# Softmax sums of heads A and B applied at the output projection of a two-layer hybrid decoder

## Chip, cores and metric

One core of one Trainium2 chip runs the whole program. The metric is device time in microseconds (us) of one execution, as the median of several runs.

## What is computed

Two decoder layers on x of shape (1, 1024, 1024), all in float32. In each layer the normalized input is projected once, and three groups of attention heads use the columns: six dilated-window heads A (width 64), six latent-attention heads B (value width 64) and four differential heads C. Their outputs stand side by side (features 0 to 383 from A, 384 to 767 from B, 768 to 1023 from C), are multiplied by `w_o` and added to x. A feed-forward block with a squared ReLU follows. What matters here:

```python
s = jnp.where(valid, s, NEG)
lse = jax.nn.logsumexp(s, axis=-1)
p = jnp.exp(s - lse[..., None])
out = jnp.einsum('bgnqk,bgnkd->bgnqd', p.astype(v.dtype), vv)
...
mixed = jnp.concatenate([out_a, out_b, out_c], axis=-1)
x = x + mixed @ w_o[layer]
```

For A and B each row of exponentials is divided by its sum. The kernel folds the three windows of A into one mask with logarithms of multiplicities, so that A, too, is one softmax for each query.

## The kernel before, in words

The function `tile_trunk` does not issue instructions. It records them (`nc` is a Recorder) with the engines on which each may run, and `Recorder.order` (line 256) then sets the order of every engine by a list schedule with a cost for each operation and a rank that is the place in the program plus a bias. The SyncE queue (SP), which issues all DMAs, is ordered by the same planner. Tiles have a tag with a fixed number of slots (`SLOTS`, line 32), and the tiles of one tag are handed out strictly in the order of the program. PSUM's eight banks are shared by the tags of `BANKS`. Matrix products are made of three passes (high by high, high by low, low by high part), so every operand is split: a "hi" copy rounded to fp32r and a "lo" difference. `WAYS` (line 50) says which engines may do each kind: `hi` is GpSimd (POOL), `lo` is VectorE (DVE) or POOL, `osum` is ScalarE (ACT), `oadd` is POOL.

A layer goes through these stages: the projection of the input (chunks of columns, most of them worked on beside the heads), 16 heads in the order A0, A1, C0 to C3, A2 to A5, B0 to B5, the output projection, and the feed-forward block.

Each head has four groups g of two query tiles i of 128 rows. `scores` (line 804) makes the products q k on TensorE (PE), subtracts from the mask and takes the row minimum on DVE, and takes the exponential on ACT, which also leaves the sum of the row (line 826). For A and B, DVE then takes the reciprocal of that sum (line 829) and POOL multiplies the row of probabilities `p` with it (kind `norm`, line 830). `values` (line 849), one group later, transposes `p` on PE (tiles `ptp`), splits it into `ph` and `pl`, and multiplies it with v into the bank `o`, of which partitions 0 to 63 and 64 to 127 hold two halves of the sum. After each second group `o_sum` (line 892) copies the two halves out with two ACT copies (`ot`, `od`), adds them on POOL and stores the 64 rows of that head to `mix_dram` with one DMA.

The output projection reads the features in blocks f of 128 (A is f = 0 to 2, B is 3 to 5, C is 6 and 7; a block holds two heads), in the groups (6, 0), (7, 1), (2, 3, 4), (5). `project_load` (line 1195) loads for each f two halves `mixr` of 128x512 with one DMA each, into the tag `pp` (5 slots, which `ph` and `pl` of the heads use as well), and splits each into `mixh` and `mixl`. The first two groups run beside the B heads. The third and fourth are loaded behind all heads in the order of the program (line 1320), and the first half of their products, for the token tiles t = 0 to 3, fills eight PSUM banks: 24 matmuls for each f, 96 in all (lines 1322 to 1329). The feed-forward block needs their sums.

Of the kernel before, what the change touches and what calls it, by code (L numbers as in the profile page):

```python
# [46 lines left out]
LAG = 3  # L47
DEEP = 6000.0

WAYS = {'hi': 'g', 'hiact': 's', 'lo': 'vg', 'lop': 'g', 'evac': 'sv', 'norm': 'g', 'osum': 's', 'oadd': 'g', 'lsc': 'gs', 'rope': 'v', 'sq': 's', 'fadd': 'gv', 'fhi': 'sg', 'flo': 'vg', 'fnorm': 'sg', 'fevac': 'sv', 'fsnap': 's', 'fsq': 'sv'}  # L50
SHARED = 0.5

BLOCKS = (0, 4, 8, 12, 15)
# [368 lines left out]
def tile_trunk(  # L422
# [21 lines left out]
    def bank(tag, name):  # L444
        return nc.tile(psum, [P, 512], F32, name, tag, BANKS[tag], True)
# [76 lines left out]
    hl_dram = nc.tile(dram, [DEPTH * NT, P, D], F32, "hl_dram")  # L522
    cq_dram = nc.tile(dram, [DEPTH * S, 512], F32, "cq_dram")
    mix_dram = nc.tile(dram, [DEPTH * D, S], F32, "mix_dram")

    def rstd_of(y, ssq, n, eps, w, nm):

# [45 lines left out]
    for L in range(DEPTH):  # L573
# [230 lines left out]
        def scores(hd, g):  # L804
# [5 lines left out]
            def piece(i, mi, z, c0, m):  # L810
# [11 lines left out]
                                               scalar=w[:, 0:1] if z else BIG, op0=ALU.add, op1=ALU.min, accum_out=w[:, z:z + 1])  # L822
                if c0 + m < W:
                    return
                tot = hd["tot"][mi][:, i] if "tot" in hd else w[:, 2:3]
                nc.scalar.activation(p, p, AF.Exp, bias=w[:, z:z + 1], scale=-1.0, accum_out=tot)
                if mi == 0:
                    if coef is None:
                        nc.vector.reciprocal(w[:, 3:4], tot)
                        copy("norm", p, p, w[:, 3:4])  # L830
                    hd["P"][g][i % 2] = p
                else:

                    prev = hd["P"][g][i % 2]
                    nc.vector.reciprocal(w[:, 3:4], tot)
                    nc.vector.scalar_tensor_tensor(w[:, 4:5], w[:, 3:4], hd["tot"][0][:, i], coef, ALU.mult, ALU.mult)
                    nc.vector.scalar_tensor_tensor(prev, p, w[:, 4:5], prev, ALU.mult, ALU.add)
# [54 lines left out]
        def o_sum(g, o, f, par, nm):  # L892

            tmp = tl("oo", [P, 512], f"ot_{nm}_{g}")
            rows = slice(64 * par, 64 * par + 64)
            dst = tl("oo", [P, 512], f"od_{nm}_{g}")[rows, :] if f < 6 else mix_tile(f, g)[rows, :]
            copy("osum", tmp[rows, :], o[64:128, :])
            copy("osum", dst, o[0:64, :])
            pair("oadd", dst, dst, tmp[rows, :], ALU.add)
            if f < 6:  # L900
                mix_out(f, g, dst, 64 * par, 64)

        def fin_mix(f, par, nm):
            return lambda g, o: o_sum(g, o, f, par, nm)

        def mask_a(W, c0, m):
            return maska[:, S - W + c0:S - W + c0 + m]
# [7 lines left out]
        def prep_a(h):  # L915
# [14 lines left out]
            def keys(cs, pt):  # L930
                hi_act(k1s[:, cs], pt)
                for z in range(2):
# [3 lines left out]
            q = turned(f"q{nm}", two(qa), lambda cs, pt: hi_act(qs[:, cs], pt))  # L936
            bl = zipped(k[0], k[1], q[0], q[1])
            return bl, dict(maps=[([(qs, k1s), (qs, k2s)], None)], mask=mask_a, scale=SC_A, nm=nm, P={},
                            v=make_v(va[:, :, c], par, nm), fin=fin_mix(i, par, nm))


        bx = {}
# [136 lines left out]
        def prep_b(h):  # L1079
            i, j = h // 2, h % 2  # L1080
            nm = f"B{L}{h}"
            qh, ql = [z[:96] for z in pairs[i][0][j]]
            kh, kl = [Halves(*z) for z in pairs[i][1][j]]
            return [], dict(maps=[([(qh, kh), (qh, kl), (ql, kh)], None)], mask=mask_c, scale=SC_B, nm=nm, P={}, cut=512,
                            v=make_v(bx["V"][:, :, 64 * h:64 * h + 64], j, nm), fin=fin_mix(3 + i, j, nm))

        cst = {}

# [106 lines left out]
        def project_load(gi):  # L1195
# [7 lines left out]
            for f in groups[gi]:  # L1203
# [4 lines left out]
                ml = tl(tag, [P, S], f"mixl_{L}_{f}", F32R)  # L1208
                for z in range(2):
                    cs = slice(z * 512, (z + 1) * 512)  # L1210
                    raw = tl("pp", [P, 512], f"mixr_{L}_{f}_{z}")
                    nc.sync.dma_start(raw, mix_dram[L * D + f * P:L * D + (f + 1) * P, cs])
                    hi_pool(mh[:, cs], raw)
                    lo_dve(ml[:, cs], raw, mh[:, cs])
                mx.append((mh, ml))
# [504 lines left out]
```

## Time and profile before

| | |
|---|---|
| median of 3 runs | 2548.02 us (2547.39 to 2551.18) |
| the profiled execution, its own time | 2549.46 us |
| its span from the first to the last instruction | 2547.7 us |
| PE busy | 2473.8 us, 97% |
| weight loads (PEld) busy | 2077.0 us, 82% |
| DVE busy | 2069.9 us, 81% |
| ACT busy | 1238.3 us, 49% |
| POOL busy | 920.2 us, 36% |
| mean granted TensorE clock | 0.991 |

The heads of the first layer run from about 65 to 587 us, those of the second from about 1320 to 1845 us. The granted clock is a share of full speed. PE's busy time is a union of pipelined instructions, each of which lasts longer than the distance to the next, so an instruction's own duration is not what it takes from PE.

### The profile page before, as it was taken

To read this page: it belongs to the slowest core of one execution; us is meant where nothing else is said; L and a number is where in the kernel's file an instruction comes from. 1 tells how busy PE (TensorE), PEld (TensorE's weight loads), DVE (VectorE), ACT (ScalarE), POOL (GpSimd) and SP (SyncE) were. 2 spreads that over 40 slices of the span, in tenths; PEclk is the share of its full clock that TensorE was granted. 3 is DMA by queue.
4 is the path that set the end of the run, shared out by engine and by line. 5 is a ranking of instruction groups with operands and counts; after the bars stand their busy time and mean duration, and the time that the engine had idled before them with its cause. 6 is when DMAs were issued, how large, how long until landed. Compare 5 with 4: busy or idle time off the path is not lost. (4 is left out here: it accounts for less than half of the span.)

```text
span 2547.7 us, 39227 instructions
## 1 busy us (share of the span) xinstructions
PE 2473.8 (97%) x12808; PEld 2077.0 (82%) x12808; DVE 2069.9 (81%) x4326; ACT 1238.3 (49%) x2548; POOL 920.2 (36%) x1078
## 2 busy tenths in 40 slices
PE   8999999999999999999999999999999999999996
PEld 7878889988788887888888778898887888788885
DVE  4679998887877777989856799988778777789989
ACT  3566667743544444323235666677345444333332
POOL 2344355653200114455323343556330001144543
PEclk9999999999999999999999999999999999999998
DMA  8354433433354457544453554344243444765332
GB/s 255 96 142 135 112 94 94 135 93 130 116 172 164 153 197 262 156 145 120 137 164 97 133 137 122 81 110 142 78 142 129 163 159 146 268 210 157 112 120 79
DMA packets 292636, 360.58 MB, mean 142 GB/s; under 512 B 48848, under 2 KB 172112, under 8 KB 292432
## 3 DMA queue, kind: packets, MB, share of 16 engines
q1 hardware_dynamic: 292432, 358.08, 45.6%
q8 instruction: 102, 1.67, 0.3%
q14 instruction: 102, 0.84, 0.1%
HBM read 231.63 MB, written 94.90 MB: 128 GB/s over the span
## 5 line engine op out<-in xcount | busy, mean ns | idle before, releaser
L418 PE MATMUL pd<-hb,ha 128*128 128x512 f32 x2520 | 577.2, 390 | 5.4 <-DVE hb L418 3.5
L418 PE MATMUL pu<-xc,uh 128*128 128x512 f32 x1792 | 552.7, 393 | 13.4 <-ACT ua L418 8.2
L418 PEld LDWEIGHTS pd<-hb,ha 128*128 128x128 f32 x2520 | 471.4, 188 | 109.6 <-DVE hb L418 8.3
L418 PEld LDWEIGHTS pu<-xc,uh 128*128 128x128 f32 x1792 | 336.9, 189 | 90.0 <-ACT ua L418 10.0
L418 PE MATMUL pu<-xc,ul 128*128 128x512 f32 x896 | 346.7, 393 | 0.0
L418 PEld LDWEIGHTS pu<-xc,ul 128*128 128x128 f32 x896 | 169.6, 189 | 36.8 <-DVE ul L418 0.8
L418 DVE TENSOR_TENSOR ha<-hr,ha 128x512 fp32r<-128x512 f32 x151 | 145.6, 967 | 24.8 <-POOL ha L418 23.0
L418 POOL TENSOR_SCALAR ha<-hr 128x512 fp32r<-128x512 f32 x90 | 74.1, 824 | 245.1 <-DVE xd L418 94.8
L418 ACT ACTIVATE hb<-wt 128x512 fp32r<-128x512 f32 x98 | 60.4, 627 | 184.4 <-PE pd L418 157.3
L418 ACT ACTIVATE uh<-su 128x512 fp32r<-128x512 f32 x124 | 77.5, 631 | 138.4 <-PE pu L418 121.6
L418 ACT ACTIVATE hb<-wd 128x512 fp32r<-128x512 f32 x82 | 50.4, 627 | 158.8 <-PE pd L418 157.3
L418 ACT ACTIVATE p_C<-p_C,w_C 128x256 f32<-128x256 f32 (+7 forms) x128 | 98.9, 773 | 55.3 <-DVE w_C L418 54.7
L418 POOL TENSOR_SCALAR p_A<-p_A,w_A 128x128 f32<-128x128 f32 (+3 forms) x96 | 77.2, 806 | 116.5 <-DVE w_A L418 83.6
L418 POOL TENSOR_SCALAR uh<-wu 128x512 fp32r<-128x512 f32 x16 | 13.3, 832 | 280.1 <-PE pu L418 168.5
L418 DVE TENSOR_TENSOR hb<-wt,hb 128x512 fp32r<-128x512 f32 x105 | 109.7, 1061 | 0.7 <-ACT hb L418 0.5
L418 DVE TENSOR_TENSOR xd<-pd,xd 128x512 f32<-128x512 f32 x128 | 86.8, 682 | 26.6 <-PE pd L418 26.5
L418 PE MATMUL pf_C<-wh_C,hh 128*128 128x512 f32 x256 | 104.7, 413 | 1.7 <-POOL wh_C L418 0.9
L418 PE MATMUL pf_C<-wl_C,hh 128*128 128x512 f32 x256 | 104.4, 408 | 0.4 <-DVE wl_C L418 0.3
L418 PE MATMUL po<-h_wo,mixh 128*128 128x512 f32 x256 | 103.3, 403 | 1.0 <-POOL h_wo L418 1.0
L418 POOL TENSOR_SCALAR p_B<-p_B,w_B 128x384 f32<-128x384 f32 (+4 forms) x96 | 74.4, 780 | 79.8 <-DVE w_B L418 62.3
L418 PE MATMUL pf_A<-wh_A,hh 128*128 128x512 f32 (+1 forms) x256 | 100.0, 395 | 3.0 <-DVE w_C L418 2.1
L418 PE MATMUL pf_C<-wh_C,hs_C 128*128 128x512 f32 x256 | 101.8, 401 | 0.7 <-DMA hs_C<-hl_dram 0.7
(343 smaller groups left out, 6775.8 us busy)
## 6 DMA issues: line engine op xcount, KB each, us to landing
hr<-hc_dram SPq DMA_DIRECT2D x210, 256.0 KB, 2.8
wu<-in_w_up_dram SPq DMA_DIRECT2D x148, 256.0 KB, 3.0
hc_dram<-hc SPq DMA_DIRECT2D x120, 256.0 KB, 2.3
wd<-in_w_down_dram SPq DMA_DIRECT2D x120, 256.0 KB, 3.7
hs_C<-hl_dram SPq DMA_DIRECT2D x32, 512.0 KB, 3.5
hs_A<-hl_dram SPq DMA_DIRECT2D x32, 512.0 KB, 3.5
hc_dram<-ua SPq DMA_DIRECT2D x60, 256.0 KB, 2.3
hl_dram<-hl SPq DMA_DIRECT2D x16, 512.0 KB, 5.6
```

The costliest lines, as they stand in the source:

```text
L418: getattr(getattr(self.nc, eng), method)(*[real(v) for v in args], **{k: real(v) for k, v in kw.items()})
```

## The change

The probabilities of A and B are no longer divided. Instead, the row sums of a head are kept in a tile `sums` of 128x8. After each fourth query tile, PE transposes four columns of it into a PSUM tile `pts` of 4x128, DVE takes the reciprocal of these 4x128 numbers, and a DMA stores them as 4 rows of 512 bytes to `rs_dram`. The bank `o` of a head is copied out by one ACT copy of 128x512, and its two halves are stored unadded by two DMAs to `half_dram`. The output projection loads, for each half of a block f below 6, the two stored halves (tags `ms` and `mx`, 2 slots each) and the reciprocals (tag `pp`, two DMAs that repeat one row of 2 KB on 64 partitions), adds the halves and multiplies with the reciprocals (kind `onorm`, DVE or POOL), and then splits as before. Blocks 6 and 7 (C) are loaded as before, but into `ms`.

```diff
--- before.py
+++ after.py
@@ -47,7 +47,7 @@
 LAG = 3
 DEEP = 6000.0
 
-WAYS = {'hi': 'g', 'hiact': 's', 'lo': 'vg', 'lop': 'g', 'evac': 'sv', 'norm': 'g', 'osum': 's', 'oadd': 'g', 'lsc': 'gs', 'rope': 'v', 'sq': 's', 'fadd': 'gv', 'fhi': 'sg', 'flo': 'vg', 'fnorm': 'sg', 'fevac': 'sv', 'fsnap': 's', 'fsq': 'sv'}
+WAYS = {'hi': 'g', 'hiact': 's', 'lo': 'vg', 'lop': 'g', 'evac': 'sv', 'onorm': 'vg', 'osum': 's', 'oadd': 'g', 'lsc': 'gs', 'rope': 'v', 'sq': 's', 'fadd': 'gv', 'fhi': 'sg', 'flo': 'vg', 'fnorm': 'sg', 'fevac': 'sv', 'fsnap': 's', 'fsq': 'sv'}
 SHARED = 0.5
 
 BLOCKS = (0, 4, 8, 12, 15)
@@ -522,6 +522,8 @@
     hl_dram = nc.tile(dram, [DEPTH * NT, P, D], F32, "hl_dram")
     cq_dram = nc.tile(dram, [DEPTH * S, 512], F32, "cq_dram")
     mix_dram = nc.tile(dram, [DEPTH * D, S], F32, "mix_dram")
+    half_dram = nc.tile(dram, [2, DEPTH * 6 * P, S], F32, "half_dram")
+    rs_dram = nc.tile(dram, [DEPTH * 12, S], F32, "rs_dram")
 
     def rstd_of(y, ssq, n, eps, w, nm):
 
@@ -822,13 +824,18 @@
                                                scalar=w[:, 0:1] if z else BIG, op0=ALU.add, op1=ALU.min, accum_out=w[:, z:z + 1])
                 if c0 + m < W:
                     return
-                tot = hd["tot"][mi][:, i] if "tot" in hd else w[:, 2:3]
+                tot = hd["tot"][mi][i] if coef is None else hd["tot"][mi][:, i]
                 nc.scalar.activation(p, p, AF.Exp, bias=w[:, z:z + 1], scale=-1.0, accum_out=tot)
                 if mi == 0:
-                    if coef is None:
-                        nc.vector.reciprocal(w[:, 3:4], tot)
-                        copy("norm", p, p, w[:, 3:4])
                     hd["P"][g][i % 2] = p
+                    if coef is None and i % 4 == 3:
+
+                        z = i // 4
+                        pt = bank("c", f"pts_{nm}_{z}")
+                        nc.tensor.transpose(pt[:4, 0:P], hd["sums"][:, 4 * z:4 * z + 4], ident)
+                        r = tl("oo", [4, P], f"rs_{nm}_{z}")
+                        nc.vector.reciprocal(r, pt[:4, 0:P])
+                        nc.sync.dma_start(rs_dram[hd["row"], z * 512:z * 512 + 512].rearrange("(t p) -> t p", p=P), r)
                 else:
 
                     prev = hd["P"][g][i % 2]
@@ -893,15 +900,25 @@
 
             tmp = tl("oo", [P, 512], f"ot_{nm}_{g}")
             rows = slice(64 * par, 64 * par + 64)
-            dst = tl("oo", [P, 512], f"od_{nm}_{g}")[rows, :] if f < 6 else mix_tile(f, g)[rows, :]
+            dst = mix_tile(f, g)[rows, :]
             copy("osum", tmp[rows, :], o[64:128, :])
             copy("osum", dst, o[0:64, :])
             pair("oadd", dst, dst, tmp[rows, :], ALU.add)
-            if f < 6:
-                mix_out(f, g, dst, 64 * par, 64)
 
         def fin_mix(f, par, nm):
-            return lambda g, o: o_sum(g, o, f, par, nm)
+            def fin(g, o):
+
+                tmp = tl("oo", [P, 512], f"ot_{nm}_{g}")
+                copy("osum", tmp, o)
+                for z in range(2):
+                    r = (L * 6 + f) * P + 64 * par
+                    nc.sync.dma_start(half_dram[z, r:r + 64, g * 512:(g + 1) * 512], tmp[64 * z:64 * z + 64, :])
+            return fin
+
+        def summed(h, f):
+
+            t = one([P, NT], "sums")
+            return dict(sums=t, tot=[[t[:, i:i + 1] for i in range(NT)]], row=(L * 6 + f) * 2 + h % 2)
 
         def mask_a(W, c0, m):
             return maska[:, S - W + c0:S - W + c0 + m]
@@ -936,7 +953,7 @@
             q = turned(f"q{nm}", two(qa), lambda cs, pt: hi_act(qs[:, cs], pt))
             bl = zipped(k[0], k[1], q[0], q[1])
             return bl, dict(maps=[([(qs, k1s), (qs, k2s)], None)], mask=mask_a, scale=SC_A, nm=nm, P={},
-                            v=make_v(va[:, :, c], par, nm), fin=fin_mix(i, par, nm))
+                            v=make_v(va[:, :, c], par, nm), fin=fin_mix(i, par, nm), **summed(h, i))
 
 
         bx = {}
@@ -1082,7 +1099,7 @@
             qh, ql = [z[:96] for z in pairs[i][0][j]]
             kh, kl = [Halves(*z) for z in pairs[i][1][j]]
             return [], dict(maps=[([(qh, kh), (qh, kl), (ql, kh)], None)], mask=mask_c, scale=SC_B, nm=nm, P={}, cut=512,
-                            v=make_v(bx["V"][:, :, 64 * h:64 * h + 64], j, nm), fin=fin_mix(3 + i, j, nm))
+                            v=make_v(bx["V"][:, :, 64 * h:64 * h + 64], j, nm), fin=fin_mix(3 + i, j, nm), **summed(h, 3 + i))
 
         cst = {}
 
@@ -1208,8 +1225,19 @@
                 ml = tl(tag, [P, S], f"mixl_{L}_{f}", F32R)
                 for z in range(2):
                     cs = slice(z * 512, (z + 1) * 512)
-                    raw = tl("pp", [P, 512], f"mixr_{L}_{f}_{z}")
-                    nc.sync.dma_start(raw, mix_dram[L * D + f * P:L * D + (f + 1) * P, cs])
+                    raw = tl("ms", [P, 512], f"mixr_{L}_{f}_{z}")
+                    if f < 6:
+                        r = slice((L * 6 + f) * P, (L * 6 + f + 1) * P)
+                        nc.sync.dma_start(raw, half_dram[0, r, cs])
+                        other, rs = tl("mx", [P, 512], f"mixo_{L}_{f}_{z}"), tl("pp", [P, 512], f"mixs_{L}_{f}_{z}")
+                        nc.sync.dma_start(other, half_dram[1, r, cs])
+                        for j in range(2):
+                            src = rs_dram[(L * 6 + f) * 2 + j:(L * 6 + f) * 2 + j + 1, cs]
+                            nc.sync.dma_start(rs[64 * j:64 * j + 64, :], src.broadcast_to([64, 512]))
+                        pair("onorm", raw, raw, other, ALU.add)
+                        pair("onorm", raw, raw, rs, ALU.mult)
+                    else:
+                        nc.sync.dma_start(raw, mix_dram[L * D + f * P:L * D + (f + 1) * P, cs])
                     hi_pool(mh[:, cs], raw)
                     lo_dve(ml[:, cs], raw, mh[:, cs])
                 mx.append((mh, ml))
```

## Rows read from the trace of the kernel before

**Rows 1.** The page's first part: busy time of each engine, its share of the span, its instructions.

```profile
PE 2473.8 (97%) x12808; PEld 2077.0 (82%) x12808; DVE 2069.9 (81%) x4326; ACT 1238.3 (49%) x2548; POOL 920.2 (36%) x1078
```

**Rows 2.** Busy time in stretches of 64 us. After the stretch: its length, then PE, PEld, DVE, ACT and POOL busy with the number of instructions, the granted clock, the DMA engines' share, GB/s. The first and the last lie where heads A2 to A5 begin in the two layers, the others in the feed-forward block.

```profile
320.00:384.00 64.00, 59.75 (x386) 55.09 (x384) 58.10 (x204) 41.56 (x91) 32.25 (x44) 0.95 0.34 96
640.00:704.00 64.00, 57.70 (x246) 45.89 (x245) 57.10 (x125) 36.88 (x73) 11.75 (x16) 0.95 0.39 124
768.00:832.00 64.00, 64.00 (x283) 52.62 (x283) 47.70 (x73) 29.02 (x48) 3.53 (x4) 1.00 0.47 157
1600.00:1664.00 64.00, 60.51 (x427) 54.21 (x425) 59.70 (x182) 46.12 (x101) 37.58 (x56) 0.97 0.30 75
```

**Rows 3.** The same view in stretches of 8 us, inside the first and the last stretch of rows 2.

```profile
368.00:376.00 8.00, 4.79 (x32) 3.46 (x32) 6.58 (x17) 5.83 (x12) 6.50 (x10) 1.00 0.24 67
376.00:384.00 8.00, 7.23 (x35) 6.44 (x34) 7.80 (x17) 4.01 (x7) 6.34 (x9) 0.57 0.39 79
...
1632.00:1640.00 8.00, 7.00 (x37) 5.58 (x37) 7.79 (x15) 3.77 (x9) 6.43 (x10) 0.79 0.29 61
```

**Rows 4.** The timeline of PE, instructions that follow a gap: start, duration, instruction, and in brackets the idle time before it and what ended it.

```profile
375.66 0.66 PE L418 MATMUL pt_kA<-ident,tm_kA 128*128 128x128 f32 x4 [1.77 <-POOL tm_kA L418]
...
1632.60 1.07 PE L418 MATMUL pt_kA<-ident,tm_kA 128*128 128x128 f32 x4 [1.77 <-POOL tm_kA L418]
```

**Rows 5.** The timeline of POOL ahead of the first gap of rows 4, merged where one instruction follows its like.

```profile
369.85 1.23 POOL L418 TENSOR_SCALAR p_A<-p_A,w_A 128x640 f32<-128x640 f32 x1
...
371.45 0.40 POOL L418 TENSOR_SCALAR tm_kA<-qkv_A 128x256 fp32r<-128x256 f32 x1
...
373.54 1.27 POOL L418 TENSOR_TENSOR od_A<-od_A,ot_A 64x512 f32<-64x512 f32 x1 [1.32 <-issue]
374.88 0.73 POOL L418 TENSOR_TENSOR tm_kA<-qkv_A,tm_kA 128x256 fp32r<-128x256 f32 x1
```

**Rows 6.** Groups of instructions that the change removes or that are nearest to those it adds: from the page (count, then busy us, mean ns of one, idle time before them) and, for `od_A` (as many again for `od_B`), from the view of that tile (duration in ns: least, median, most).

```profile
L418 POOL TENSOR_SCALAR p_A<-p_A,w_A 128x128 f32<-128x128 f32 (+3 forms) x96 | 77.2, 806 | 116.5 <-DVE w_A L418 83.6
L418 POOL TENSOR_SCALAR p_B<-p_B,w_B 128x384 f32<-128x384 f32 (+4 forms) x96 | 74.4, 780 | 79.8 <-DVE w_B L418 62.3
L418 DVE RECIPROCAL w_A<-w_A 128x1 f32<-128x1 f32 x96 | 14.8, 155 | 15.3 <-ACT p_A L418 14.8
L418 DVE RECIPROCAL ci<-tot 128x8 f32<-128x8 f32 x8 | 1.5, 188 | 0.0
L418 ACT ACTIVATE od_A<-o_A x24: 577/591/592, 98.1 to 1701.6; 64x512 f32<-64x512 f32 x24
L418 POOL TENSOR_TENSOR od_A<-od_A,ot_A x24: 1266/1286/1621, 99.1 to 1702.3; 64x512 f32<-64x512 f32 x24
```

**Rows 7.** Transpositions on PE: sixteen in a row and the matmul behind them (timeline), and all those of the A heads (groups of PE).

```profile
617.57 1.91 PE L418 MATMUL ptu<-ident,xr 128*128 128x128 f32 x16
619.23 0.48 PE L418 MATMUL po<-h_wo,mixh 128*128 128x512 f32 x1
...
L418 PE MATMUL ptp_A<-ident,p_A 128*128 128x128 f32 x432 | 78.1, 280 | 1.7 <-POOL p_A L418 1.5
```

**Rows 8.** Who waited for the tiles `p_A` and `p_B`: weight loads of their transpositions (us in all, times).

```profile
  PEld ptp_A L418: 5.6, 13
...
  PEld ptp_B L418: 2.3, 6
```

**Rows 9.** The loads of the output projection: all of them from the page of DMA issues (KB each, median us to landing) and from the view of the tile `mixr` (ns), and, from the timeline of SP and ACT at the end of the first layer's heads, the first loads of the third group and the last `ph`.

```profile
mixr<-mix_dram SPq DMA_DIRECT2D x32, 256.0 KB, 3.4
...
L418 POOL TENSOR_SCALAR mixh<-mixr x32: 611/822/1093, 522.8 to 1853.5; 128x512 fp32r<-128x512 f32 x32
L418 DVE TENSOR_TENSOR mixl<-mixr,mixh x32: 676/994/1100, 523.9 to 1855.0; 128x512 fp32r<-128x512 f32 x32
...
584.01 3.11 SPq L418 DMA_DIRECT2D mixr<-mix_dram  x5
...
584.59 0.49 ACT L418 ACTIVATE ph_B<-ptp_B 128x384 fp32r<-128x384 f32 x1 [1.89 <-PE ptp_B L418]
```

**Rows 10.** The products of the output projection: the timeline of PE (two neighbours, and the one gap), the timeline of DVE (the last sum of the second group, the first of the third), and what all `po` instructions took of PE in the last 16 us of the heads (stretch, length, PE busy, PEld busy, DVE busy, clock, DMA).

```profile
596.35 0.50 PE L418 MATMUL po<-h_wo,mixh 128*128 128x512 f32 x1 [0.58 <-POOL h_wo L418]
...
609.40 0.39 PE L418 MATMUL po<-h_wo,mixh 128*128 128x512 f32 x1
609.63 0.39 PE L418 MATMUL po<-l_wo,mixh 128*128 128x512 f32 x1
...
591.12 0.68 DVE L418 TENSOR_TENSOR xr<-po,xr 128x512 f32<-128x512 f32 x1
...
608.93 4.09 DVE L418 TENSOR_TENSOR xr<-po,xr 128x512 f32<-128x512 f32 x6 [7.23 <-PE po L418]
...
613.69 0.69 DVE L418 TENSOR_TENSOR xr<-po,xr 128x512 f32<-128x512 f32 x1
...
568.00:584.00 16.00, 11.56 (x41) 6.82 (x40) 4.61 (x7) 1.00 0.28 86
```

**Rows 11.** Gaps of PE in the feed-forward block and the clock behind them: timeline, and stretches of 5 us.

```profile
667.50 0.73 PE L418 MATMUL pu<-xc,uh 128*128 128x512 f32 x2 [2.25 <-ACT ua L418]
...
672.37 0.73 PE L418 MATMUL pu<-xc,uh 128*128 128x512 f32 x2 [1.83 <-ACT ua L418]
...
680.00:685.00 5.00, 5.00 (x16) 3.94 (x16) 3.57 (x8) 1.05 (x2) 0.00 (x0) 0.66 0.36 106
```

## Prediction

> **What bounds the kernel now.** I read the busy times first, then the table of stretches, then the gaps of the engine that bounds. PE is busy for 97% of the span [rows 1], so the time is PE's work plus 74 us of gaps (2547.7 - 2473.8) plus what PE loses where its granted clock falls. The stretches show where those losses are. In the feed-forward block PE is busy for all of 64 us, or loses time to its own chains [rows 2, 11], which the change doesn't touch. In the stretches where heads A2 to A5 begin, PE stands idle for 4.25 and 3.49 us and the clock is at 0.95 and 0.97 [rows 2]. The finer table puts most of that into a few microseconds: 3.2 us of gaps from 368 to 376, and then a clock of 0.57, which is mostly the lower level of 1.2 GHz, from 376 to 384; in the second layer 0.79 [rows 3]. So a change that relieves POOL, DVE or ACT can earn no more than these gaps and what the clock gives back with them, while each instruction added to PE costs its full time.
>
> **What the change removes.** There are 24 heads of A and B (12 in each layer), hence 192 rows of probabilities, 48 outputs `o` and 24 halves of 128x512 at the output projection.
> POOL loses 192 scalings, 77.2 + 74.4 = 151.6 us, and 48 additions of 1.29 us, 62 us [rows 6]. ACT loses one of two copies for each `o`: 48 x 0.59 = 28 us [rows 6]. DVE loses 192 reciprocals of one column, 192 x 0.155 = 30 us [rows 6]. None of these engines bounds the kernel, so their sums aren't gains. The gain is what PE waited for them:
> (a) Transpositions that waited for POOL's scaling: 1.5 us of PE's idle time in A [rows 7]. The weight loads waited 5.6 and 2.3 us [rows 8], but most of that lay beside running matmuls. I take 1.5 of a possible 7.9.
> (b) Two gaps of 1.77 us, one in each layer, ended by POOL's `tm_kA` [rows 4]. POOL's timeline says why: between the hi copy at 371.45 and the subtraction at 374.88 stands an addition `od_A` of 1.27 us that had waited 1.32 us, and ahead of them a scaling of 1.23 us [rows 5]. Without these, `tm_kA` can run more than 1.77 us earlier. What is late next is DVE, busy 6.58 and 7.80 of 8 us there [rows 3]. I take 3.5 us for both layers; it is 0 if the planner fills POOL's free time with differences `lo` taken from DVE.
> (c) The clock behind these gaps: 8 x 0.43 = 3.4 us and 8 x 0.21 = 1.7 us lie below full clock [rows 3]. Other gaps beside them stay, so I take half, 2.6 of 5.1.
> Sum: -7.6, between 0 and -16.5 (7.9 + 3.5 + 5.1).
>
> **What it adds to PE.** 48 transpositions of `sums`. Sixteen transpositions in a row begin at 617.57 and the matmul behind them at 619.23 [rows 7], some 0.11 us for each with the last one's overlap ((1.91 - 0.27) / 15). The A heads' 432 take 78.1 us, 0.18 for each [rows 7]. So 48 cost 5.3 us, at most 8.7. I take 5.3, since neighbours overlap in the interleaved order too. One transposition lasts 0.28 us [rows 7], and were PE to pay that, 48 would be 13.4 us, 8 more; that is a rival below.
> The Trainium skill speaks for that rival: "TensorE: Matmul & The Clock Gate", Part 4: PE-mode transpose, gives about 275 ns to a 128x128 transposition inside a kernel. By that the 48 would cost 13.2 us. The trace agrees with 275 ns as a duration, but sixteen took 1.91 us, so it isn't what PE pays in a row.
> Each new transposition also waits for ACT's exponential of a fourth row, and the next scores and transpositions queue behind it on PE. The planner puts it late enough by its own costs; what these miss shows in the old waits on `p`: 5.6 + 2.3 us for 192 rows [rows 8], 2.0 for 48, of which part is covered. I take 1 (0 to 5).
>
> **What it adds elsewhere.** DVE gets 48 reciprocals of 128 columns. One column takes 155 ns and eight take 188 [rows 6], some 5 ns for each more, so 0.76 us each, an estimate, and 36 us in all. On DVE, the row minima behind such a reciprocal wait for PE's transposition; the next exponentials would wait for these. With the 30 us removed the balance is small, and I cost it at nothing: PE's matmuls of the older group cover it. Without that cover it is one reciprocal on the path of each half head, 48 x 0.76 = 36 us, which no row supports. The bank of `pts` is held for one such reciprocal; `o` is released one ACT copy earlier. Together nothing.
> SP gets 48 stores of sums (in its queue they wait for DVE, ahead of head stores and key moves), 48 more stores of outputs and 72 more loads. At 3.11 / 5 = 0.62 us each [rows 9] that is 104 us of issuing over two layers of heads, beside PE's work.
> The output projection is where I expect to pay. Each half now needs four DMAs, two `onorm` operations, hi and lo, and its two stored halves sit in tags of two slots instead of five. So the two halves of one f must be finished before the next f can be loaded: 1.24 us to issue two loads, 3.4 us to land, about 2 x 0.9 for `onorm`, 0.82 for hi and 0.99 for lo [rows 9], 8.25 us for each f. PE uses up one f in 24 x 0.227 = 5.4 us [rows 10]. Besides, the reciprocals go to `pp`, which comes free with the last `ph`, at about 584 [rows 9].
> Beside the heads (f = 0 and 1) scores and values cover it. Behind them, PE works on `po` from about 591 to 613.5, with one gap of 0.58 [rows 10]. If the reciprocals of f = 2 are asked for at 584, they land at 588 and f = 2 is done at 590.7. Then hi of f = 3 is there at 598, of 4 at 606.2, of 5 at 614.5, while PE would want them at 596.5, 601.9 and 607.3. The last ends 5.4 later, at 620 instead of 613.5: 6.5 us in each layer.
> Against that: the second group's own loads get slower by such a turn, too, so its matmuls, 11.6 of 16 us at the end of the heads [rows 10], move back and leave PE to the heads. The heads then end earlier, by up to 8.25 x 11.56 / 16 = 6 us, the shorter chain of the last group (one scaling, 1.2 us) helps, and matmuls that moved back fill the wait. So between 0 and 6.5 for each layer; I take 2, 4 for both.
>
> **Sum.** -7.6 + 5.3 + 1 + 4 = +2.7 us. The profiled execution took 2549.46, so 2552.2 by its own time; the median of the runs is 1.4 lower, so 2550.7, say 2551. A difference of 0.2% (5 us) is about what a measurement of this kernel tells from no change, so this counts as the same.
>
> **The rivals.**
> R1, the relief reaches further. All idle time and all clock of the two stretches comes back: 4.25 + 3.49 from gaps, and 64 x 0.05 + 64 x 0.03 = 5.1 from the clock [rows 2], with (a) 14.3. The output projection costs nothing, since the heads end early. 5.3 + 1 - 14.3 = -8, 2540. For it: POOL loses 214 of its 920 us, and its additions stand in the gap. Against it: DVE is busy 58 and 60 of 64 us there and hardly gets less.
> R2, slower: the two slots starve PE behind the heads. If the last `ph` stays at 584 and the second group keeps its place, PE waits 6.5 us in each layer, with gaps of 1.5 to 3 us. In the feed-forward block two gaps of 2.25 and 1.83 us came before a stretch at a clock of 0.66 [rows 11], so I add up to 1.5 us for each layer. 5.3 + 1 - 7.6 + 13 + 2 = +14, 2562. It decides as soon as an f takes longer than 5.4 us and less than one f of matmuls is left behind the heads. For it: the sum of durations; against it: the planner's freedom to move the second group.
> R3, the change doesn't do what it says: POOL's free time is filled with work moved from DVE and the `tm_kA` gaps stay. Only (a) is gained: 5.3 + 1 + 4 - 1.5 = +9, 2557.
> R4, each new transposition costs PE its whole 0.28 us: 8 more, 2559.
>
> **How the numbers follow.** Forecast 0.40, R1 0.25, R2 0.24, R3 0.07, R4 0.04. The time is the forecast's, 2551; its own range is 2546 to 2556, by the halves of the terms that I left open. The range from 2537 to 2563 takes in R1, R3, R4 and R2's time, and leaves out what lies beyond, some 2 in 10. Faster by over 0.2% is R1, 0.25; slower is R2, R3 and R4, 0.35; the forecast is within.
>
> **What would show it.** Right: 48 transpositions `pts` at about 0.11 us of PE; no gap on `tm_kA` where A2 begins, and a clock near 1.00 there; POOL some 200 us less busy; a turn of about 8 us from one f to the next on `mixo` and `mixr`, and gaps of 0 to 4 us of PE on `mixh` behind the heads. Wrong: gaps of over 5 us there (R2), none there and no gaps in the heads (R1), gaps on `pts`, or new gaps at places that the old trace doesn't show, since the planner orders everything anew.

## The result and the profile after

The changed kernel takes 2572.99 us in the median of its runs (2570.90 to 2576.53), against 2549.60 us for the kernel before in the same session: a ratio of 1.0096, 95% interval 1.0076 to 1.0116. One of the four runs of the kernel before took 5947.85 us; it counts in its median (2548.02 without it) but not in the ratio, and two such runs of other sessions (6311.83 of the kernel before, 3062.15 of p1) are in no ratio either. By the ratio the changed kernel is slower by 24.5 us, and its median lies beyond the range's upper end of 2563. The profiled execution took 2574.39 us, its span is 2572.3.

The page's busy times, as in [rows 1]:

```profile
PE 2482.5 (97%) x12856; PEld 2083.1 (81%) x12856; DVE 2091.9 (81%) x4238; ACT 1203.3 (47%) x2494; POOL 698.1 (27%) x836
```

POOL is relieved by 222 us and PE has 48 instructions more, both as foretold. DVE is busier by 22 us, although it lost 192 reciprocals. To see where the time went I cut each layer at marks that both traces have: the last `pj` (products of all heads begin to be prepared), the first `ptkr` (from here the heads are those of A and B alone), the last `o_B` (the heads end), the first `pu` (the feed-forward block begins). The tables show the busy time of each engine in these stretches, with columns as in [rows 2]; length less PE's busy time is PE's idle time. Before:

```profile
61.33:384.22 322.89, 309.40 (x1781) 263.00 (x1780) 269.95 (x781) 198.31 (x481) 139.73 (x199) 0.98 0.42 116
384.22:586.14 201.92, 200.64 (x1394) 180.07 (x1393) 165.03 (x443) 130.63 (x284) 107.34 (x135) 1.00 0.39 106
586.14:641.47 55.33, 54.31 (x265) 44.71 (x264) 41.61 (x98) 22.51 (x43) 21.64 (x28) 1.00 0.44 148
1323.29:1640.73 317.44, 305.90 (x1780) 259.19 (x1778) 266.81 (x770) 195.81 (x472) 137.69 (x199) 0.99 0.42 117
1640.73:1842.37 201.64, 200.57 (x1393) 180.18 (x1394) 165.62 (x444) 130.75 (x284) 107.09 (x135) 1.00 0.37 104
1842.37:1897.57 55.20, 54.38 (x265) 44.70 (x264) 41.63 (x98) 22.51 (x43) 21.50 (x28) 1.00 0.44 148
```

And after:

```profile
60.88:385.79 324.91, 309.72 (x1790) 262.43 (x1789) 268.36 (x761) 194.29 (x473) 104.94 (x161) 0.98 0.42 118
385.79:592.82 207.03, 201.89 (x1408) 181.20 (x1408) 173.78 (x405) 119.50 (x263) 35.96 (x55) 1.00 0.45 127
592.82:654.24 61.42, 56.17 (x249) 44.85 (x248) 47.20 (x107) 19.05 (x42) 16.50 (x24) 0.94 0.59 188
1338.19:1656.08 317.89, 306.95 (x1790) 260.36 (x1789) 263.07 (x750) 191.82 (x465) 105.44 (x161) 0.99 0.43 119
1656.08:1862.58 206.50, 201.72 (x1408) 181.33 (x1409) 173.32 (x405) 119.37 (x263) 35.45 (x55) 1.00 0.44 125
1862.58:1921.74 59.16, 54.76 (x248) 44.01 (x247) 47.31 (x107) 19.04 (x42) 16.22 (x24) 0.97 0.59 196
```

The reader is to see three things. The heads of A and B are 5.1 and 4.9 us longer, with 3.9 and 3.7 us more of PE's idle time; DVE has 9 and 8 us more to do there and POOL a third of what it had. The projection is 6.1 and 4.0 us longer, with 4.2 and 3.6 us more idle time and a lower clock. Together that is 20.0 of the 24.6 us between the spans. The first stretch, in which [rows 4] had their two gaps, isn't shorter: its idle time in the two layers is 13.5 + 11.5 = 25.0 us before and 15.2 + 10.9 = 26.1 after.

What PE waited for after the change: the largest groups whose waits are new, and last the one that the change was foretold to shorten. It is there once, at 70 us where A0 begins, instead of at the three places of before (us in all, times, longest):

```profile
PE po L418 <- POOL mixh L418: 11.5, 7, 2.8
...
PE o_A L418 <- DVE pl_A L418: 4.0, 8, 1.0
...
PE ptp_B L418 <- DVE pl_B L418: 2.4, 4, 1.0
...
PE pt_kA L418 <- POOL tm_kA L418: 2.2, 1, 2.2
```

The same view of the first layer's first stretch alone, two rows before and two after:

```profile
PE pt_kA L418 <- POOL tm_kA L418: 3.9, 2, 2.2
...
PE ptp_A L418 <- POOL p_A L418: 1.1, 2, 0.8
```

```profile
PE s_C L418 <- DMA qs_C<-qs_C: 2.2, 1, 2.2
...
PE s_C L418 <- DVE w_C L418: 1.7, 4, 0.7
```

Adding up all gaps over 0.15 us in the first stretches of both layers, those that end on POOL fall from 8.8 to 2.9 us, but those that end on DVE rise from 7.1 to 12.2, and those that end on a DMA from 0.7 to 4.8.

The timeline of PE after: a new transposition among matmuls, a wait for `pl` in the heads, and two waits in the first layer's projection (start, duration, instruction, idle time before it and what ended it):

```profile
387.98 0.28 PE L418 MATMUL pqr<-wqrh,lath 128*128 128x192 f32 x1
388.10 0.27 PE L418 MATMUL pts_A<-ident,sums 128*4 128x128 f32 x1
388.12 0.34 PE L418 MATMUL pqr<-wqrl,lath 128*128 128x192 f32 x1
388.30 0.27 PE L418 MATMUL pqr<-wqrh,latl 128*128 128x192 f32 x1
...
392.10 0.39 PE L418 MATMUL o_A<-pl_A,vhl_A 128*128 128x256 f32 x1 [0.97 <-DVE pl_A L418]
...
606.08 0.50 PE L418 MATMUL po<-h_wo,mixh 128*128 128x512 f32 x1 [2.78 <-POOL mixh L418]
...
616.07 0.50 PE L418 MATMUL po<-h_wo,mixh 128*128 128x512 f32 x1 [2.28 <-POOL mixh L418]
```

The timeline of DVE, ahead of that wait for `pl`, and behind the heads: the projection's first multiply, the last use of a buffer and the addition on what is loaded into it next:

```profile
389.07 0.94 DVE L418 RECIPROCAL rs_A<-pts_A 4x128 f32<-4x128 f32 x1
...
390.11 0.54 DVE L418 COPY qr<-pqr 128x384 f32<-128x384 f32 x1
...
391.37 0.67 DVE L418 TENSOR_TENSOR pl_A<-ptp_A,ph_A 128x512 fp32r<-128x512 f32 x1
...
593.93 0.69 DVE L418 TENSOR_TENSOR mixr<-mixr,mixs 128x512 f32<-128x512 f32 x1 [1.59 <-DMA mixs<-rs_dram]
...
608.39 0.68 DVE L418 TENSOR_TENSOR mixl<-mixr,mixh 128x512 fp32r<-128x512 f32 x1
...
613.89 0.69 DVE L418 TENSOR_TENSOR mixr<-mixr,mixo 128x512 f32<-128x512 f32 x1 [0.99 <-DMA mixr<-half_dram]
```

The transposition takes about 0.1 us of PE's stream: the matmuls `pqr` start 0.11 apart elsewhere in that row, but two such steps, from 387.98 to 388.30, take 0.32 with the transposition among them, 0.10 more. But the reciprocal behind it holds DVE for 0.94 us, and `pl`, for which PE then idles, comes out of the same queue. All 48 of them, in the groups of DVE (busy us, mean ns):

```profile
L418 DVE RECIPROCAL rs_B<-pts_B 4x128 f32<-4x128 f32 x24 | 22.6, 942 | 2.2 <-PE pts_B L418 1.8
L418 DVE RECIPROCAL rs_A<-pts_A 4x128 f32<-4x128 f32 x24 | 22.6, 941 | 10.1 <-PE pts_A L418 10.1
```

The timeline of SP after, at the end of the first layer's heads and behind them:

```profile
567.78 1.53 SPq L418 DMA_DIRECT2D mixr<-half_dram  x2
...
575.70 0.32 SPq L418 DMA_DIRECT2D mixo<-half_dram  x1
...
585.79 0.27 SPq L418 DMA_DIRECT2D rs_dram<-rs_B  x1
...
590.45 4.30 SPq L418 DMA_DIRECT2D mixs<-rs_dram  x7
...
609.11 0.33 SPq L418 DMA_DIRECT2D mixr<-half_dram  x1
```

What SP waited for from 585 to 592 us, the longest:

```profile
SPq L418 <- DVE pl_B L418: 3.4, 1, 3.4
```

The halves of f = 2 were asked for at 568 to 576, the reciprocals that divide them only at 590.45: the buffers `pp` that they load into are still held by the heads, whose last `pl` SP waits for. I call this the gate. So the first turn of the projection behind the heads begins with the multiply at 593.93, and not at 588 or earlier. The turns behind it are long as well: PE's second wait, up to 616.07, is for a half whose load leaves at 609.11, as soon as `mixl` (608.39 to 609.07) has set its slot free, and is there for the addition at 613.89.

### The profile page after: what moved, and what is told of

Read it like the earlier page. It is cut to its first block, busy times and chain, and to the rows that moved or that the text cites. A ratio compares the mean times of both kernels' runs of the same rounds, so it can differ in the third digit from the quotient of the medians.

```text
span 2572.3 us, 38972 instructions
## 1 busy us (share of the span) xinstructions
PE 2482.5 (97%) x12856; PEld 2083.1 (81%) x12856; DVE 2091.9 (81%) x4238; ACT 1203.3 (47%) x2494; POOL 698.1 (27%) x836
## 5 line engine op out<-in xcount | busy, mean ns | idle before, releaser
L418 PE MATMUL po<-h_wo,mixh 128*128 128x512 f32 x256 | 106.0, 414 | 11.5 <-POOL mixh L418 11.5
L418 ACT ACTIVATE p_B<-p_B,w_B 128x128 f32<-128x128 f32 (+3 forms) x96 | 74.3, 774 | 65.3 <-DVE w_B L418 64.8
L418 PE MATMUL po<-l_wo,mixh 128*128 128x512 f32 x256 | 103.3, 403 | 0.0
L418 PE MATMUL po<-h_wo,mixl 128*128 128x512 f32 x256 | 101.7, 407 | 0.4 <-DVE mixl L418 0.4
```

The lines of the kernel that those rows point to most:

```text
L418: getattr(getattr(self.nc, eng), method)(*[real(v) for v in args], **{k: real(v) for k, v in kw.items()})
```

## The experiments

Theories. T1: the reciprocals. 48 x 0.94 us on DVE, for which I had charged nothing, push `pl` back and starve PE in the heads. T2: the projection. R2 of the prediction, slots and gate starve PE behind the heads. T3: PE's own added work. T4: nothing of the division, but the halves stored apart and the new order of the whole plan. "Heads and projection" is the sum of those two stretches over the first and the second layer; the kernel before has 257.3 and 256.8 us, the changed one 268.5 and 265.7. All ratios are to the kernel before on the same chip; since the kernels ran on several chips, I compare them with each other by the column "loss", which is ratio less 1 by 2549 us, and not by their medians. By the intervals a loss is known to 2 to 5 us (the changed kernel's is 19.4 to 29.6), e8's to 7.

| kernel | median us | ratio, 95% interval | loss us | heads and projection us |
|---|---|---|---|---|
| changed | 2572.99 | 1.0096, 1.0076 to 1.0116 | 24.5 | 268.5, 265.7 |
| e1_recip | 2564.46 | 1.0060, 1.0043 to 1.0077 | 15.3 | 263.9, 262.9 |
| e2_zfirst | 2576.78 | 1.0102, 1.0088 to 1.0116 | 26.0 | 267.0, 267.3 |
| e3_both | 2571.30 | 1.0079, 1.0066 to 1.0092 | 20.1 | 263.1, 265.9 |
| e5_cost | 2570.56 | 1.0078, 1.0065 to 1.0092 | 19.9 | 268.3, 267.0 |
| e6_rstmp | 2566.56 | 1.0061, 1.0048 to 1.0074 | 15.5 | 263.5, 262.3 |
| e7_recip_rstmp | 2562.51 | 1.0045, 1.0031 to 1.0059 | 11.5 | 261.6, 260.2 |
| e8_direct | 2719.60 | 1.0676, 1.0649 to 1.0703 | 172.3 | 316.3, 325.4 |
| e9_pts5 | 2575.44 | 1.0107, 1.0094 to 1.0120 | 27.3 | 263.7, 262.9 |
| e10_nodiv | 2551.73 | 1.0010, 1.0001 to 1.0019 | 2.5 | 255.4, 254.6 |
| p1_halves | 2551.41 | 1.0005, 0.9996 to 1.0014 | 1.3 | 258.5, 256.8 |
| p2_sums | 2569.02 | 1.0079, 1.0066 to 1.0092 | 20.1 | 267.9, 268.6 |
| p9_rawtmp | 2550.86 | 1.0008, 0.9999 to 1.0017 | 2.0 | 257.5, 258.4 |

**The two halves of the change alone.** p1 is the kernel before with outputs stored as two halves that are added at the projection, and the division left on the probabilities. p2 has the sums' path, with the halves added on POOL as before.

```diff
 p1, against the changed kernel
-                    if coef is None and i % 4 == 3:   (transposition, reciprocal, store)
+                        nc.vector.reciprocal(w[:, 3:4], tot)
+                        copy("norm", p, p, w[:, 3:4])
-                        pair("onorm", raw, raw, rs, ALU.mult)
 p2, against the changed kernel
+            return lambda g, o: o_sum(g, o, f, par, nm)
-                        pair("onorm", raw, raw, other, ALU.add)
```

> The kernel before with one part of the change: the two halves of an output are stored apart, loaded into ms and mx and added at the output projection; the division stays on the probabilities, so no sums, no transpositions, no reciprocals of 128 columns and no pp gate. By my theory the heads cost what they did or a little less, and the projection at most 1 to 2 us in each layer: 2546 to 2554. If the two slots of ms and mx, or the doubled loads, are the cost behind the heads, 2557 or more.

> The other part alone: the sums are transposed, inverted, stored and multiplied in at the output projection as in the change, but the halves are added on POOL and stored as one, so each half of a block is one load and one multiplication. By my theory nearly all of the loss is here: the long reciprocals (5 us in each layer) and the gate of pp, whose turns are shorter with one load (2 to 4 us in each layer): 2563 to 2570. If the halves are the cost, 2556 or less.

p1 can't be told from before, p2 carries 20 of the 24.5 us. So the loss lies in the sums, and the halves stored apart have little part in it.

**The reciprocal ahead of the transposition (T1).** On `sums`, 128 partitions x 4, it needs four columns, not 128; a copy out of PSUM takes its place behind the transposition. The work for PE is the same.

```diff
+                        rc = one([P, 4], "rc")
+                        nc.vector.reciprocal(rc, hd["sums"][:, 4 * z:4 * z + 4])
-                        nc.tensor.transpose(pt[:4, 0:P], hd["sums"][:, 4 * z:4 * z + 4], ident)
+                        nc.tensor.transpose(pt[:4, 0:P], rc, ident)
-                        nc.vector.reciprocal(r, pt[:4, 0:P])
+                        copy("evac", r, pt[:4, 0:P])
```

> Takes the reciprocals of the 128x4 sums before the transposition (four columns on DVE, some 0.17 us, and a copy of 4x128 on ACT or DVE behind it) instead of the 4x128 after it (0.94 us measured on DVE, where the planner reckons with 0.2). If the long reciprocals delay DVE's queue and with it PE between heads (my theory for the 5 us that each layer loses between the key transposition ptkr and the last o_B), each layer gets 3 to 5 us back there: 2563 to 2567 against the 2573 of the change. If instead the 24 transpositions, the new order or the DMA traffic cost the heads, it stays within 3 us of 2573.

The loss falls by 9.2 us (by the two intervals together, 3 to 16). The view of the tile `rc` in e1 (ns, least, median, most) and the stretches of the heads in both layers:

```profile
L418 DVE RECIPROCAL rc<-sums x48: 164/173/180, 89.6 to 1846.1; 128x4 f32<-128x4 f32 x48
```

```profile
388.10:590.64 202.54, 200.90 (x1411) 182.82 (x1409) 161.13 (x407) 122.18 (x276) 38.00 (x57) 0.99 0.46 129
...
1650.82:1854.54 203.72, 200.91 (x1411) 182.65 (x1409) 161.37 (x407) 121.94 (x276) 38.18 (x57) 0.99 0.45 126
```

DVE has 12 us less in each layer's heads than in the changed kernel, and PE's idle time there falls from 5.14 and 4.78 to 1.64 and 2.81 us (1.28 and 1.07 before the change). The heads are 4.5 and 2.8 us shorter, the projection stays at 61.3 and 59.2. T1 holds for the heads, with 7.3 us. The two traces differ elsewhere, too: the first stretches are 2.3 and 1.0 us longer, and what has neither heads nor their projection is 6 us shorter, though the edit doesn't touch it.

**The planner's price.** The planner charges 202 ns for such a reciprocal (69 + 1.04 x 128). e5 tells it 940, with no instruction changed, so that it may place them better.

```diff
+            if method == "reciprocal" and n > 8:
+                return 940.0
```

> The kernel with the change, the planner alone is told that a reciprocal of 128 columns takes 0.94 us and not 0.2. The same instructions in another order. If it is the misplacing that delays PE, as much comes back as with the short reciprocals, 3 to 5 us for each layer, 2563 to 2567. If it is DVE's time itself, 2570 to 2574.

The loss falls from 24.5 to 19.9, with intervals that overlap, and heads and projection stay (268.3 and 267.0). So the cost is mostly DVE's time, and at most in part an ignorant plan.

**The order of the loads (T2, a miss).** e2 loads token half 0 of all four last f first, so that a turn needs no other half. e3 adds e1's edit.

```diff
-            for f in groups[gi]:
-                for z in range(2):
+            for z in range(2):
+                for k, f in fs:      (all f of both last groups)
-        most, last = project_load(2), project_load(3)
+        most, last = project_load(2, 3)
```

> Only the loads behind the heads change their order: first token half 0 of blocks 2, 3, 4, 5, then token half 1. The first 96 matmuls need only half 0, so two turns of the two slots bring them instead of four. If the two slots starve PE (gaps on mixh of 2.78 + 2.28 and 2.48 + 1.74 us, and a clock of 0.79 beside them), these gaps fall under 1 us each and the time by 7 to 10 us, to 2563 to 2566. If the transfers themselves are too slow (bandwidth: 285 GB/s and a DMA share of 0.95 were seen there), the gaps stay at 2 us or more and the time above 2569.

> Both of the edits before. If the two causes are separate, their gains add: 2553 to 2560, still not under the kernel before, for which PE's 5.3 us of transpositions stand. If it is the new order as such, no more than the better of the two alone.

Both failed to shorten the projection (60.6 and 61.1 us in e2, 59.9 and 61.2 in e3), and e3 isn't better than e1 alone. In e2 PE's two large waits on `mixh` became smaller, 1.2 and 0.9 us in the first layer instead of 2.8 and 2.3, but smaller waits came beside them, and its idle time is 4.4 and 5.1 us. e2's timeline of SP shows what the order doesn't touch: the reciprocals are asked for as late as in the changed kernel, whatever is loaded first.

```profile
590.04 4.99 SPq L418 DMA_DIRECT2D mixs<-rs_dram  x7
```

So a better order of the turns behind the gate brings nothing; what is left to try is the gate itself. The other outcome that e2's expectation names, transfers that are too slow, isn't excluded: the DMA engines' share is 0.85 and 0.91 from 600 to 616 us in the changed kernel and 0.96 from 600 to 608 in e2, where the kernel before has at most 0.70 in stretches of 8 us from 576 to 608. No run separates slow transfers from long turns.

**The gate (T2, mended).** e6 loads the reciprocals into the three buffers of `tmp` instead of `pp`, one word; e7 is e6 with e1's edit.

```diff
-other, rs = tl("mx", ...), tl("pp", [P, 512], f"mixs_{L}_{f}_{z}")
+other, rs = tl("mx", ...), tl("tmp", [P, 512], f"mixs_{L}_{f}_{z}")
```

> One word changes: the loaded reciprocals go to the tag tmp (three slots that nothing uses during the B heads) instead of pp. In the trace of the change they were asked for at 590.45, when the last pl of the heads set pp free, though the two stored halves of block 2 had been there since about 578. If this gate is what starts the turns of the two slots too late (my theory after the reordered loads brought nothing), blocks 2 to 4 are loaded, or partly so, beside the last heads, the gaps on mixh behind the heads go, and each layer gets 4 to 6 us back: 2562 to 2566. If the turn itself (8 us for each block) or the bandwidth is the limit, at most 2 us in each layer: 2569 or more.

> The short reciprocals and the tag tmp together. If long reciprocals in the heads and the gate of pp are the two causes, 2552 to 2557: what is left over the kernel before is the 5.3 us of transpositions on PE less what POOL's relief gives. If the two overlap, or if the new order costs by itself, 2560 or more.

e6 gains 9.0 us (3 to 15 by the intervals). Its stretches of heads and projection, both layers:

```profile
389.04:598.13 209.09, 203.34 (x1407) 181.41 (x1408) 182.09 (x420) 119.47 (x263) 47.98 (x66) 1.00 0.51 146
598.13:652.56 54.43, 53.99 (x264) 44.80 (x263) 37.32 (x93) 21.90 (x42) 13.80 (x20) 1.00 0.43 142
...
1652.77:1860.62 207.85, 202.85 (x1407) 181.29 (x1408) 181.98 (x420) 119.36 (x263) 47.35 (x66) 1.00 0.50 144
1860.62:1915.09 54.47, 54.03 (x264) 44.78 (x263) 37.00 (x93) 21.91 (x42) 13.73 (x20) 1.00 0.43 143
```

The projection is 7.0 and 4.7 us shorter, below that of the kernel before, at full clock and with 0.44 us of idle time: with an early gate the two slots suffice. A late gate alone isn't the cause either: the kernel before loads into the same `pp`, from 584.01 [rows 9], 2.1 us ahead of its heads' end, and with five slots and one load for each half PE is idle for 1.0 and 0.8 us in its projection. It takes both, a late gate and long turns behind it. In e6 the additions and multiplies run beside the heads: DVE has 182 us of work there where it had 174, and the heads grow by 2.1 and 1.4 us. Of that only 0.6 and 0.2 us are idle time of PE, so that it is a wait for DVE isn't shown. The gains of e1 and e6 don't add up in the losses (9.2 + 9.0, and 13.0 measured in e7), but with such intervals that isn't clear of noise; in the traces e7's heads are 4.7 and 2.0 us longer than e1's.

**What is left in e7, 11.5 us over the kernel before.** e9 issues each transposition of e7 five times; e8 stores `rc` without any; e10 leaves out the whole path from the sums.

```diff
 e9
-nc.tensor.transpose(pt[:4, 0:P], rc, ident)
+nc.tensor.transpose(pt[:4, 0:P], rc, ident)      (five times)
 e8
-pt = bank("c", f"pts_{nm}_{z}")      (with transposition and copy)
-nc.sync.dma_start(rs_dram[...].rearrange("(t p) -> t p", p=P), r)
+nc.sync.dma_start(rs_dram[...].rearrange("(t p) -> p t", p=P), rc)
 e10, against the changed kernel
-                    if coef is None and i % 4 == 3:      (transposition, reciprocal, store)
-                        for j in range(2):               (loads of the reciprocals)
-                        pair("onorm", raw, raw, rs, ALU.mult)
```

> As e7, with each of the 48 transpositions issued five times, into the same bank: 192 more on PE. By the 0.11 us from start to start that the stream shows they add 21 us, to 2580 to 2588; by the 0.27 us that one lasts, 52 us, to 2610 to 2620; if they lie in gaps of PE, under 5 us.

> As e7, but without the 48 transpositions: the reciprocals, taken token by token from the accumulated sums, are stored straight from their 128 x 4 tile, in pieces of 4 bytes. e7 took 2562.5 us, with PE idle 3.9 us in the stretch of A's and B's heads and the stretch 5.3 us longer than before. If the rest of the loss is the work of the transpositions on PE (24 per layer at 0.11 us, 2.6 us, and 5 us in both layers) and the waits for their PSUM bank and copy, the time falls to 2553 to 2559 us and the stretch to 202 to 205 us. If the transpositions cost nothing and the rest is the new order of the plan, it stays at 2560 to 2565. If short pieces are what the rows of 512 bytes were meant to avoid, the loads of the reciprocals behind the heads come later and the projection grows past 54.4 us per layer.

> The changed kernel without the whole path of the reciprocals: no transposition, no reciprocal, no store, no load and no multiply; the probabilities stay undivided, so the division is left out of the computation. The sums are still accumulated into their own tile and the halves stored apart. e7, the best of the changed kernels, stays at 2562.5 us, 14 above the kernel before. If these instructions carry the rest, the time falls to 2545 to 2553, the heads to 202 to 204 us and the projection to 54 us, as where only the halves were stored apart (2551.4). If it is the accumulation of the sums, or what the plan does with POOL free of 96 scalings per layer, it stays at 2557 to 2565.

e9: 192 more transpositions cost 15.8 us, 0.08 each, less than I expected by either price, and part of them fell into gaps (PE's idle time in the heads fell from 3.9 and 3.9 us to 1.8 and 0.9). By that the change's 48 are worth 3.9 us, by their 0.11 in the stream 5.3.

e8 loses 160 us more than e7 and doesn't answer its question. Its timelines of SP, ACT and PE in the first layer, and stretches of 4 us:

```profile
379.39 0.38 SPq L418 DMA_DIRECT2D rs_dram<-rc  x1
380.79 0.92 SPq L418 DMA_DIRECT2D cc<-cq_dram  x2
```

```profile
391.20 0.91 ACT L418 ACTIVATE cc<-cc,rl 128x384 f32<-128x384 f32 x2 [8.37 <-DMA cc<-cq_dram]
```

```profile
392.64 1.11 PE L418 MATMUL ptl<-ident,cc 128*128 128x128 f32 x4 [8.02 <-ACT ot_A L418]
```

```profile
384.00:388.00 4.00, 0.61 (x2) 0.30 (x2) 2.40 (x6) 0.00 (x0) 0.79 (x1) 0.99 0.27 33
388.00:392.00 4.00, 0.00 (x0) 0.00 (x0) 0.00 (x0) 0.80 (x2) 0.13 (x1) 0.50 0.34 75
```

A store of 2 KB is issued at 379.39, and the load of `cc` behind it at 380.79 lands only at 391.2; ACT and then PE stand still for 8 us, and the clock falls to 0.50. In e7 the same loads, issued at 368.76 and 1.0 us behind the store of rows, are used from 371.48. The page of e8's profile counts 329113 packets, 24960 more than in e7, and 48 stores of 512 pieces of 4 bytes are 24576. So the rows of 512 bytes, for which the change transposes at all, are worth their transpositions. The Trainium skill, "DMA: Bandwidth & Descriptors", Specifications, gives 512 B as the least transfer at line rate and read-modify-write below it; the trace agrees in direction, and what it adds is that the loads behind such a store pay.

e10, the division left out, is at 2551.73. Its stretches:

```profile
59.03:386.77 327.74, 311.20 (x1786) 264.70 (x1785) 265.47 (x752) 194.38 (x473) 106.43 (x164) 0.97 0.43 118
386.77:587.66 200.89, 197.98 (x1391) 179.71 (x1390) 163.89 (x394) 120.27 (x266) 39.54 (x61) 1.00 0.48 136
587.66:642.12 54.46, 54.02 (x264) 44.81 (x263) 36.29 (x92) 21.91 (x42) 13.66 (x20) 1.00 0.43 143
```

So transposition, reciprocal, store, load and multiply carry 22.0 of the 24.5 us; e7 takes away 13.0 of these and leaves 9.0. And the opposite is as telling: even with no division anywhere, with 192 scalings taken off POOL and 192 reciprocals off DVE, the kernel isn't faster than before (ratio 1.0010). Heads and projection gain 1.9 us in this layer, and the first stretch gives 4.9 back (2.3 and 2.9 in the second). e10 still stores the halves apart, but that doesn't hide a gain: p1 does so too and divides on the probabilities, and its loss is 1.3 us, not more than e10's 2.5.

**A version that beats both?** p9 takes e6's lesson to the kernel before, whose loads also go to `pp` (`tmp` has three slots and `pp` five, not two each as the expectation says).

```diff
-                    raw = tl("pp", [P, 512], f"mixr_{L}_{f}_{z}")
+                    raw = tl("tmp", [P, 512], f"mixr_{L}_{f}_{z}")
```

> The kernel before with one word changed: the loads behind the heads go to the two buffers of tmp and not to the two of pp, which the last transpositions of the heads hold. The projection took 55.3 and 55.2 us there with 1.0 and 0.8 us of PE idle at its start; with an earlier gate it falls to 54.0 to 54.5, so 1 to 2.5 us are gained and the time is 2546 to 2549. If the wait at the gate is nothing here, or the plan moves other work by as much, it stays at 2549 to 2552.

The projection fell to 54.4 us in both layers as expected, the heads grew by 1.2 and 2.3 us, and the time is the same. None of the kernels beats the one before.

## Why the prediction was wrong, point by point

- **The gain of 7.6 us, "(a)" to "(c)", wasn't there.** The mechanism was read rightly as far as POOL goes: where [rows 4] show gaps on `tm_kA`, none is left, and the clock behind them comes back in part (0.95 and 0.84 in the two stretches of 8 us from 368 to 384, and, in the second layer, 1.00 from 1624 to 1664). But the idle time of the first stretch stayed (25.0 and 26.1), and p1 and e10, which differ in the division (and in the tile that keeps the sums), show no gain from taking it away (losses of 1.3 and 2.5). I had counted gaps that end on POOL as time to be had; gaps that end on DVE and on a DMA took their place (12.2 instead of 7.1 us, 4.8 instead of 0.7). "(b)" names DVE as what is late next and takes 3.5 us all the same. This is the first step that failed.
- **The transpositions, 5.3 us, were right**: 0.11 us each in the stream, 3.9 us in all by e9's slope. R4, 0.28 each, is wrong.
- **The reciprocals: "I cost it at nothing: PE's matmuls of the older group cover it."** This is the second step that failed. One takes 0.94 us, not the 0.76 of my estimate from [rows 6] (from one column to 128 it grows by (942 - 155) / 127 = 6.2 ns a column, not 5), and the cover isn't there: they stand in the queue ahead of `pl`, for which PE waits. e1 puts 9.2 us on them, 7.3 of which its trace shows in the heads. I had named the price of no cover, 36 us, and then said that no row supports it, instead of taking a part of it into the range.
- **The projection: "between 0 and 6.5 for each layer; I take 2".** This is the third step that failed. It measured 6.1 and 4.0 in its stretch, and e6 earns 9.0 us of time. I argued that the heads would end earlier and that moved matmuls would fill the wait. The heads ended later, at 592.82 instead of 586.14, and the gate moved with them: I took it at 584, and it was 590.45, 2.4 us ahead of the heads' end. Behind the gate the first turn took what the terms say, once they are added up rightly. By the sum's own terms the first hi copy is there at 591.3 (584 + 1.24 + 3.4 + 1.8 + 0.82), not at 589.7, and that of f = 3 one turn later at 599.5, which is 15.5 us behind the gate. PE's wait for it ended at 606.08, 15.6 behind the gate. The next turn took 10.0 us, to 616.07, instead of 8.25.
- **R2 had the sign, the mechanism and nearly the size** of the projection's part (13 us; it was 10): a gate at the end of the heads, and two slots behind it. What it had wrong was the rest: it stood on the -7.6 that didn't come and left out the reciprocals. R2 without these two errors is 5.3 + 1 + 13 + 2 + 9 = 30; measured are 24.5.
- **What stays open** is how the 9 us between e7 and e10 divide. The transpositions are 4 to 5 of them by e9 and the stream; the rest is shared by copies, multiplies on DVE, 48 stores and 48 loads. e8 was to tell and was spoiled by its short pieces. In e7 the clock falls to 0.79 in two of the 8 us stretches of the first layer's heads, some 3 us, which e10's heads don't show; but e10 has one such fall just ahead of them (0.79 from 376 to 384), so at most half of that belongs here.

## What to carry to other kernels

A reciprocal is paid by the column: take it where the numbers lie across partitions, before they are turned into rows, and price what is queued behind it on its engine. When a load gets a new tag, ask first who holds that tag last, since this decides the start of the next stage; a late start that cost 1 us a layer with five slots cost 4 to 6 us a layer with two slots and three more transfers for each half. And whether taking work off an engine earns anything, as POOL's scalings here didn't, is best found out by leaving the work out before anything is built to replace it.

## What was not expected of the hardware

- DVE's reciprocal takes 155 ns for 1 column, 173 for 4, 188 for 8 and 942 for 128, the last on 4 partitions and from PSUM, the others on 128: 6.2 ns for each more column, where other DVE work on 512 columns takes 670 to 690 ns, 1.3 a column. The Trainium skill, "VectorE: DVE Perf Modes", First, the fixed hardware budget, says that it runs as an iterative divide with a repeat count of 8. An estimate from that and the page's 0.96 GHz is 128 x 8 / 0.96 = 1.07 us; the trace agrees within 0.13 us (0.94), and my 0.76 from two rows was further off. By the column it doesn't agree: 6.2 ns are measured, and 8 / 0.96 would be 8.3.
- Behind one store of 512 pieces of 4 bytes, a load issued 1.4 us later landed 10.4 us after its issue (at most 2.7 us behind a store of rows, in e7), and 48 of them make the kernel 160 us longer than 48 stores of rows.
- Four partitions of output make a transposition no shorter (272 ns), and no dearer in the stream.
